# Hybrid encoder block, output part of its ConvFFN: the sums for the last product's weights released one by one during the product s3

## The chip, the cores and the metric

The kernel runs on one core of one Trainium2 chip. The metric is the device time of one execution in microseconds (us); the time of a kernel is the median of its runs. Engines: PE (matmul), PEld (its weight loads), DVE (VectorE), ACT (ScalarE), POOL (GpSimd) and SP (SyncE, here used only to issue transfers).

## What is computed

The reference is a streaming-encoder block on x of 512 x 1024 float32: an RWKV-7 branch and an RG-LRU branch merged by gates, a cross-attention into 256 memory rows, then a gated ConvFFN with inner width 2816, and a last norm. The change touches the ConvFFN's second product, with w_out of 2816 x 1024:

```
def conv_ffn(h, w_in, conv_w, conv_b, w_out):
    u = h @ w_in
    gate = causal_dwconv(u[..., :D_FF], conv_w, conv_b)
    return (jax.nn.gelu(gate) * u[..., D_FF:]) @ w_out

x = x + conv_ffn(rms_norm(x, norm_ffn_g[l]), w_ffn_in[l], ffn_conv_w[l], ffn_conv_b[l], w_ffn_out[l])
return rms_norm(x, norm_final_g)
```

## The kernel before

**The output product in seven products.** The product with w_out is done in Strassen's way (the form with seven products). Its weight matrix is cut into four quarters by input half and output half, its other operand into four quarters by input half and half of the 512 positions. The products run in the order A11, A12, s1, s2, s3, A22, s4 (`out_weights`, L1333). Those with an A take a quarter of w_out itself; those with an s take sums of quarters. Each product has 4 output tiles m times 11 input tiles k = 44 blocks. A block is one 128x128 weight tile against 256 positions. Both factors are split into a high and a low part, and a block is three matmuls (`mm3`, L169 to L173): high by high (L170), high by low (L171), low by high (L172). PSUM tiles are `ox_ps` (X: A11, s2, s3, A22) and `oyz_ps` (YZ: A12, s1, s4).

**The weights of the sums.** They are made in DRAM by transfers, not on an engine: `dO[n, m]` gets one quarter by a copy, and a second one by a transfer that adds to what is there (`accum_op`). POOL's queue issues them (`out_sums`, L518 to L536; the transfers are L521 and L530). s4 has no buffer of its own. Its weights are those of s2 plus one more quarter, added in place in `dO["s2", m]` once the weights of s2 have been read from there:

```
else:
    yield from runs("s2", m, 1, 2, **add)          # L536: n == "s4"
```

`out_runs` cuts a row of 11 blocks wherever a stored piece of 8 blocks ends. For s4 that gives 2, 2, 3 and 2 transfers for m = 0 to 3, nine in all, of 64 to 512 KB, 2816 KB together.

**Pacing.** The generator `sums` (L551) holds all sums of this kind up to s3. `sum_behind(ins)` (L177) takes the next one and lets it wait, by a semaphore, for the matmul `ins`; earlier stages of the kernel call it, and so does the first output product, A11, for its first 12 blocks (L1449). Sums are kept in the order of the program in POOL's queue. The nine sums for s4 are issued by a plain loop between s2 and s3 (L1461), with no pace: each waits only for the loads that read the s2 weights that it overwrites.

**The stream of weights.** `out_weights` packs the 308 blocks of the seven products, in order, into weight tiles of 8 blocks (128x1024, 512 KB). For each of them SP loads a raw tile `wfo_r` (L1354, one transfer or several; four buffers), ACT casts it to the high part `wfo_h` (L1357), DVE makes the low part `wfo_l` (L1358); three buffers each for high and low. Numbered from 0, s2 has tiles 16.5 to 22, s3 22 to 27.5, A22 27.5 to 33, s4 33 to 38.5. Loads of an A product read w_out in DRAM (`in_wfo`), those of an s product read `dO` (shown as `dOs` in the profile).

**Other work around it.** Before a product its second operand is split into high and low by ACT and DVE (`split_g`, L1248 and L1249, tiles `go`); the operand of A22 is built at L1465. As an output tile is finished, DVE and ACT add it to the residual `xr`: s2 at L1460, s3 and A22 and s4 in `ffn_out` (L1395 to L1405).

Of the kernel before, what the change touches and what calls it, by code (L numbers as in the profile page):

```python
# [12 lines left out]
ALU = mybir.AluOpType  # L13
# [45 lines left out]
def hybrid_block_kernel(ctx: ExitStack, tc: tile.TileContext, xT_d, mT_d, pv_d, cst_d, win_d, wk_d, wv_d,  # L59
# [29 lines left out]
    def par(name, i, n=1):  # L89
        o = PV[name][0]  # L90
        return pv[:, o + i:o + i + n]
# [49 lines left out]
    class Units:  # L141
# [10 lines left out]
        def next(self):  # L152
            if self.left == 0:
                self.fill()
            i = self.i
            self.i += 1
            self.left -= 1
            return self.hi[:, i * P:(i + 1) * P], self.lo[:, i * P:(i + 1) * P]
# [10 lines left out]
    def mm3(ps, lh, ll, rh, rl, start, stop, **kw):  # L169
        first = PE.matmul(ps, lh, rh, start=start, stop=False, **kw)  # L170
        PE.matmul(ps, lh, rl, start=False, stop=False, **kw)  # L171
        PE.matmul(ps, ll, rh, start=False, stop=stop, **kw)  # L172
        return first  # L173

    sums = iter(())

    def sum_behind(ins, n=1):  # L177

        for put in islice(sums, n):
            tc.add_manual_dep(tc.keep_in_program_order(put()).ins, ins.ins.name, mybir.DependencyInfo(  # L180
                mybir.DependencyClass.Sync, mybir.DependencyReason.DATA), reason="pace of the sums")
# [293 lines left out]
    def w_sums():  # L475
        def put(b, out, src, acc=True):
            def s(name):
                return dS[b][:, :, SLOT[name], :].rearrange("n p f -> p n f")

            if type(src) is tuple:  # L480
                src = quarter(b * NQ, *src, n=NQ)
            else:
                src = s(src)
            kw = dict(accum_op=ALU.add) if acc else {}
            return lambda: nc.gpsimd.dma_start(s(out), src, **kw)  # L485

        nb = FB // NQ
        for b in range(nb + 1):
            for k in range(4):
                if b < nb:  # L490
                    yield (put(b, "s1", (2, 1), False), put(b, "s1", (2, 2)),
                           put(b, "s3", (2, 1), False), put(b, "s3", (1, 1)))[k]
                if b and k < 2:
                    yield (put(b - 1, "s4", "s2", False), put(b - 1, "s4", (1, 2)))[k]
                elif b < nb and k > 1:
                    yield (put(b, "s2", "s1", False), put(b, "s2", (1, 1)))[k - 2]


    HB = FB // 2
    MQ = KB // 2  # L500

    def out_units(m, r, c):

        return [divmod(((r - 1) * MQ + m) * FB + (c - 1) * HB + k, 8) for k in range(HB)]

    def out_runs(units):

        k = 0
        while k < len(units):
            p, i = units[k]  # L510
            n = min(len(units) - k, 8 - i)
            yield k, n, wfo_d[p, :, i * P:(i + n) * P]
            k += n
# [4 lines left out]
    def out_sums(names):  # L518
        def runs(n, m, r, c, **kw):
            for k, w, src in out_runs(out_units(m, r, c)):  # L520
                yield lambda k=k, w=w, src=src: nc.gpsimd.dma_start(dO[n, m][:, k * P:(k + w) * P], src, **kw)  # L521

        add = dict(accum_op=ALU.add)
        for n in names:
            for m in range(MQ):
                if n == "s1":
                    yield from runs(n, m, 2, 1)
                    yield from runs(n, m, 2, 2, **add)
                elif n == "s2":
                    yield lambda m=m: nc.gpsimd.dma_start(dO["s2", m], dO["s1", m])  # L530
                    yield from runs(n, m, 1, 1, **add)
                elif n == "s3":
                    yield from runs(n, m, 2, 1)
                    yield from runs(n, m, 1, 1, **add)
                else:
                    yield from runs("s2", m, 1, 2, **add)  # L536
# [14 lines left out]
    sums = chain(w_sums(), out_sums(("s1", "s2", "s3")))  # L551
# [189 lines left out]
    with tc.tile_pool(name="pz", bufs=1, reuse_waits="tile") as pz:  # L741
# [9 lines left out]
        for s in range(30, -1, -1):  # L751
            n = 31 - s
# [25 lines left out]
    for i0 in (0, 16):  # L778
# [3 lines left out]
        for i in range(16):  # L782
            for e in range(2):
                r, k = rows[0][e], rows[1][e]
                PE.matmul(psh[e][k, i * 32:(i + 1) * 32], BZ[r, i0 + i, 32:64], ZA[r, i0 + i, :],
                          start=True, stop=True)
        for e, copy in enumerate((S.copy, V.tensor_copy)):
            k = rows[1][e]
            copy(Hs[e][k], psh[e][k].rearrange("p (i t) -> p i t", t=32))
        for i in range(16):  # L790
            for e in range(2):
                r, k = rows[0][e], rows[1][e]
                PE.matmul(pso[e][r, i * 32:(i + 1) * 32], Hs[e][k, i, :], BZ[k, i0 + i, 32:64],
                          start=True, stop=True)
# [384 lines left out]
    for m in order:  # L1179
# [5 lines left out]
        i = m % 4  # L1185
# [60 lines left out]
    def split_g(i, src, k):  # L1246
        dst, n = part(i, k)
        S.copy(dst[:, :, 0, :], src(slice(k, k + n)))  # L1248
        V.tensor_tensor(dst[:, :, 1, :], src(slice(k, k + n)), dst[:, :, 0, :].bitcast(F32), ALU.subtract)  # L1249

    def g1(ks, c):
        return graw[:, ks, (c - 1) * H:c * H]
# [15 lines left out]
    for m0 in range(0, FB, NQ):  # L1268
        ms = range(m0, m0 + NQ)
        YZ = {m: pf.tile([P, T], F32, tag="yz", name=f"fyz_ps{m}", bufs=4) for m in ms}  # L1270
        X = {m: pf.tile([P, T], F32, tag="x", name=f"fx_ps{m}", bufs=4)[:, 0:H] for m in ms}
        sn = {m: pc.tile([P, T], F32, tag="sn", name=f"sn{m}", bufs=3) for m in ms}
        p5 = {m: pc.tile([P, H], F32, tag="p5", name=f"p5_{m}", bufs=3) for m in ms}
# [14 lines left out]
        elif m0 // NQ <= KB:  # L1288
            k = m0 // NQ - 1
# [13 lines left out]
        for m in ms:  # L1303
# [9 lines left out]
            out = graw[:, m]  # L1313
            V.scalar_tensor_tensor(out[:, 0:H], X[m], -1.0, ac[:, 0:H], ALU.mult, ALU.mult)
            V.scalar_tensor_tensor(out[:, H:T], p5[m], -1.0, ac[:, H:T], ALU.mult, ALU.mult)
            k = m % HB
# [44 lines left out]

    uf = out_weights()

    def out_product(n, i, out, start, done, nsum=0):

        for m, k in out_order:
            wh, wl = next(uf)
            g = gsets[i][k // 8][:, k % 8]
            ins = mm3(out[m], wh, wl, g[:, 0, :], g[:, 1, :], start and k == 0, k == HB - 1,
                      skip_group_check=not start)  # L1370
            if m * HB + k < nsum:
                sum_behind(ins)
            if k == HB - 1:
                done(m)
# [9 lines left out]
    X = [pf.tile([P, T], F32, tag="x", name=f"ox_ps{m}", bufs=4)[:, 0:H] for m in range(MQ)]  # L1384
    YZ = [pf.tile([P, T], F32, tag="yz", name=f"oyz_ps{m}", bufs=4) for m in range(MQ)]
    cols = (slice(0, H), slice(H, T))
    sn1, sn5 = ([pc.tile([P, T], F32, tag="sn", name=f"{n}_{i}", bufs=3) for i in range(2)] for n in ("o1", "o5"))
    p1, p5 = ([t[:, c] for t in ts for c in cols] for ts in (sn1, sn5))

    def ffn_out(src, snap, sign, m, ts, last=False):  # L1390

        n = ts.stop - ts.start
        if snap is not None:
            t1 = pc.tile([P, T], F32, tag="s", name=f"t1_{m}_{ts.start}")
            V.tensor_tensor(t1[:, :n], src, snap, ALU.add)  # L1395
            src = t1[:, :n]
        V.tensor_tensor(xr[:, m, ts], xr[:, m, ts], src, sign)
        sq = pc.tile([P, T], F32, tag="ac", name=f"t2_{m}_{ts.start}")[:, :n]
        S.activation(sq, xr[:, m, ts], AF.Square)
        if last:  # L1400
            V.tensor_scalar(xr[:, m, ts], xr[:, m, ts], par("nfin", m), None, ALU.mult)
        else:
            S.activation(xr[:, m, ts], xr[:, m, ts], AF.Identity, scale=par("nfin", m))
        if not last:
            V.tensor_tensor(sso[:, ts], sso[:, ts], sq, ALU.add)  # L1405
        return sq
# [40 lines left out]
    prepare(1, lambda ks: g2(ks, 1))  # L1447
    prepare(2, lambda ks: g1(ks, 1))
    out_product("A11", 0, X, True, lambda m: S.copy(p1[m], X[m]), 12)  # L1449
    for k in K4:  # L1450
        ks = slice(k, min(k + 4, HB))
        V.scalar_tensor_tensor(g1(ks, 1), g2(ks, 2), -1.0, g1(ks, 1), ALU.mult, ALU.subtract)
        split_g(0, lambda ks: g1(ks, 1), k)
    out_product("A12", 1, [t[:, 0:H] for t in YZ], True,
                lambda m: ffn_out(YZ[m][:, 0:H], p1[m], ALU.add, m, cols[0]))
    prepare(1, lambda ks: g2(ks, 2))
    out_product("s1", 2, [t[:, H:T] for t in YZ], True, lambda m: S.copy(p5[m], YZ[m][:, H:T]))
    prepare(2, lambda ks: g1(ks, 2))
    out_product("s2", 0, X, False,
                lambda m: V.tensor_tensor(xr[:, m, cols[1]], xr[:, m, cols[1]], X[m], ALU.add))  # L1460
    for put in out_sums(("s4",)):  # L1461
        tc.keep_in_program_order(put())
    for k in K4:
        ks = slice(k, min(k + 4, HB))
        V.scalar_tensor_tensor(g1(ks, 1), g1(ks, 1), -1.0, g2(ks, 1), ALU.mult, ALU.subtract)  # L1465
        split_g(0, lambda ks: g1(ks, 1), k)
    out_product("s3", 2, X, False, lambda m: ffn_out(X[m], p5[m], ALU.subtract, MQ + m, cols[1]))
    out_product("A22", 0, X, False, c21)
    out_product("s4", 1, [t[:, H:T] for t in YZ], False, c12)

# [76 lines left out]
```

## Time and profile before

| | us |
|---|---|
| timed runs | 885.95, 889.65, 891.37 |
| median | 889.65 |
| profiled execution, its own time | 888.2 |
| its span, first to last instruction | 886.4 |
| PE busy | 865.9 (98%) |
| DVE busy | 676.7 (76%) |
| ACT busy | 513.6 (58%) |
| POOL busy | 132.5 (15%) |

Times in the profile are us from the start of the span. A row of instructions gives start, duration, engine, line, operation, output <- inputs, and in brackets the idle time of the engine before it with what ended that. A matmul lasts longer than the distance to the next one, since matmuls are pipelined: the pace is read from the starts. Transfers have a time to landing, from issue until their data is in place. Queue q0 is POOL's, q1 is SP's; they share 16 DMA engines.

### The profile page before, as it was taken

To read this page: it belongs to the slowest core of one execution; us is meant where nothing else is said; L and a number is where in the kernel's file an instruction comes from. 1 tells how busy PE (TensorE), PEld (TensorE's weight loads), DVE (VectorE), ACT (ScalarE), POOL (GpSimd) and SP (SyncE) were. 2 spreads that over 40 slices of the span, in tenths; PEclk is the share of its full clock that TensorE was granted. 3 is DMA by queue.
4 is the path that set the end of the run, shared out by engine and by line. 5 is a ranking of instruction groups with operands and counts; after the bars stand their busy time and mean duration, and the time that the engine had idled before them with its cause. 6 is when DMAs were issued, how large, how long until landed. Compare 5 with 4: busy or idle time off the path is not lost.

```text
span 886.4 us, 15940 instructions
## 1 busy us (share of the span) xinstructions
PE 865.9 (98%) x6197; PEld 755.0 (85%) x6197; DVE 676.7 (76%) x1096; ACT 513.6 (58%) x788; POOL 132.5 (15%) x163
## 2 busy tenths in 40 slices
PE   8999999999999999999989999999999999999996
PEld 7778878888877677888867778999999999999896
DVE  6796598777967777685565568898888788998674
ACT  7575676643337676243454456766665566767563
POOL 0101222021101012001112211112111211111100
PEclk9999999999999999999999999999999999999999
DMA  8878899678997379858877868899999999998963
GB/s 279 301 254 215 209 223 238 191 197 240 260 236 156 74 197 230 229 157 239 220 205 169 203 150 191 239 258 285 300 257 297 262 320 277 249 280 207 293 208 95
DMA packets 97562, 201.37 MB, mean 227 GB/s; under 512 B 19600, under 2 KB 30992, under 8 KB 97424
## 3 DMA queue, kind: packets, MB, share of 16 engines
q1 hardware_dynamic: 62240, 118.57, 40.5%
q0 software_dynamic: 25504, 67.38, 37.3%
q10 hardware_dynamic: 9744, 14.42, 4.9%
q8 instruction: 48, 0.79, 0.4%
q14 instruction: 26, 0.21, 0.1%
HBM read 188.54 MB, written 78.12 MB: 301 GB/s over the span
## 4 chain that ended last, share of the span: by engine, by line
PE 80%; DMA 8%; DVE 7%; ACT 3%; issue 1%; ACTq 0%; SPq 0%; DVEq 0%
PE in_ps L171 7%; PE in_ps L172 7%; PE in_ps L170 7%; PE fx_ps L170 3%; PE fx_ps L172 3%; PE fx_ps L171 3%; PE fyz_ps L170 3%; PE fyz_ps L171 3%; PE fyz_ps L172 3%; DMA wfi_r<-in_wfi 2%; DMA wfo_r<-dOs 2%; PE co_ps L172 2%; PE mix_ps L171 2%; PE co_ps L171 2%; PE mix_ps L170 2%; PE co_ps L170 2%
## 5 line engine op out<-in xcount | busy, mean ns | idle before, releaser
L171 PE MATMUL in_ps<-hT,win_h 128*128 128x512 f32 x304 | 121.0, 398 | 0.4 <-DVE hT L387 0.4
L172 PE MATMUL in_ps<-hT,win_l 128*128 128x512 f32 x304 | 121.3, 399 | 0.0
L170 PE MATMUL in_ps<-hT,win_h 128*128 128x512 f32 x304 | 120.5, 398 | 0.3 <-DVE pr L589 0.3
L136 ACT CAST wfi_h<-wfi_r 128x1024 fp32r<-128x1024 f32 x77 | 80.9, 1051 | 64.4 <-PE fyz_ps L171 17.2
L137 DVE TENSOR_TENSOR wfi_l<-wfi_r,wfi_h 128x1024 fp32r<-128x1024 f32 x77 | 93.9, 1220 | 23.5 <-ACT wfi_h L136 23.4
L485 POOL DMA_DIRECT2D dS<-in_wfi x66 | 66.7, 1034 | 299.2 <-PE in_ps L170 96.4
L171 PEld LDWEIGHTS in_ps<-hT,win_h 128*128 128x128 f32 x304 | 57.1, 188 | 14.6 <-DVE hT L387 1.0
L170 PEld LDWEIGHTS in_ps<-hT,win_h 128*128 128x128 f32 x304 | 57.1, 188 | 13.4 <-DVE pr L589 0.7
L172 PEld LDWEIGHTS in_ps<-hT,win_l 128*128 128x128 f32 x304 | 57.1, 188 | 12.9 <-issue 0.7
L521 POOL DMA_DIRECT2D dOs<-in_wfo x54 | 39.8, 784 | 171.3 <-PE fx_ps L170 46.0
L123 DVE TENSOR_TENSOR win_l<-win_r,win_h 128x1024 fp32r<-128x1024 f32 x38 | 46.3, 1220 | 24.1 <-ACT win_h L122 20.6
L122 ACT CAST win_h<-win_r 128x1024 fp32r<-128x1024 f32 x38 | 39.9, 1050 | 40.0 <-PE in_ps L171 35.6
L1358 DVE TENSOR_TENSOR wfo_l<-wfo_r,wfo_h 128x1024 fp32r<-128x1024 f32 (+1 forms) x39 | 46.9, 1206 | 14.4 <-ACT wfo_h L1357 14.4
L1357 ACT CAST wfo_h<-wfo_r 128x1024 fp32r<-128x1024 f32 (+1 forms) x39 | 40.3, 1035 | 30.3 <-DMA wfo_r<-dOs 14.0
L172 PE MATMUL ox_ps<-go,wfo_l 128*128 128x256 f32 x176 | 48.8, 277 | 1.2 <-DVE wfo_l L1358 1.2
L170 PE MATMUL ox_ps<-go,wfo_h 128*128 128x256 f32 x176 | 48.7, 277 | 0.6 <-ACT wfo_h L1357 0.6
L170 PE MATMUL fx_ps<-hr,wfi_h 128*128 128x256 f32 x176 | 48.7, 277 | 0.3 <-ACT sn L1293 0.3
L170 PE MATMUL fx_ps<-hq,wfi_h 128*128 128x256 f32 x176 | 48.8, 277 | 0.1
L172 PE MATMUL fyz_ps<-hq,wfi_l 128*128 128x256 f32 x176 | 48.7, 277 | 0.0
L172 PE MATMUL fx_ps<-hq,wfi_l 128*128 128x256 f32 x176 | 48.7, 277 | 0.0
L170 PE MATMUL fyz_ps<-hq,wfi_h 128*128 128x256 f32 x176 | 48.7, 277 | 0.0
L171 PE MATMUL fx_ps<-hq,wfi_h 128*128 128x256 f32 x176 | 48.6, 276 | 0.0
(432 smaller groups left out, 2689.7 us busy)
## 6 DMA issues: line engine op xcount, KB each, us to landing
dS<-in_wfi POOLq DMA_DIRECT2D x66, 512.0 KB, 7.6
wfi_r<-dS SPq DMA_DIRECT2D x44, 512.0 KB, 6.9
win_r<-in_win SPq DMA_DIRECT2D x38, 512.0 KB, 5.3
wfi_r<-in_wfi SPq DMA_DIRECT2D x33, 512.0 KB, 5.6
dS<-dS POOLq DMA_DIRECT2D x22, 512.0 KB, 5.7
dOs<-in_wfo POOLq DMA_DIRECT2D x12, 512.0 KB, 7.8
wk_r<-in_wk SPq DMA_DIRECT2D x8, 512.0 KB, 5.8
wv_r<-in_wv SPq DMA_DIRECT2D x8, 512.0 KB, 5.2
```

The lines of the kernel that those rows point to most:

```text
L122: casts.append(S.copy(hi[:, o:o + n], raw[:, o:o + n]))
L123: V.tensor_tensor(lo[:, o:o + n], raw[:, o:o + n], hi[:, o:o + n].bitcast(F32), ALU.subtract)
L136: S.copy(hi, raw)
L137: V.tensor_tensor(lo, raw, hi.bitcast(F32), ALU.subtract)
L170: first = PE.matmul(ps, lh, rh, start=start, stop=False, **kw)
L171: PE.matmul(ps, lh, rl, start=False, stop=False, **kw)
L172: PE.matmul(ps, ll, rh, start=False, stop=stop, **kw)
L485: return lambda: nc.gpsimd.dma_start(s(out), src, **kw)
L521: yield lambda k=k, w=w, src=src: nc.gpsimd.dma_start(dO[n, m][:, k * P:(k + w) * P], src, **kw)
L1357: S.copy(hi[:, :n], raw[:, :n])
L1358: V.tensor_tensor(lo[:, :n], raw[:, :n], hi[:, :n].bitcast(F32), ALU.subtract)
```

## The change

The nine sums for s4 are no longer issued between s2 and s3. They are put behind what is left in `sums`, and the product s3 releases them: `out_product` gets an argument `every`, and with `every=3` the blocks 0, 3, 6, ... of s3, counted over its 44 blocks, release one sum each, until `nsum` have been released. `nsum` is `len(late)`, the count of the sums for s4, nine by the code above, so block 24 releases the last. What would be left in `sums` then is issued after s3. The short description of the change speaks of ten transfers; the code gives nine.

```
-    def out_product(n, i, out, start, done, nsum=0):
+    def out_product(n, i, out, start, done, nsum=0, every=1):
...
-            if m * HB + k < nsum:
+            if (m * HB + k) % every == 0 and (m * HB + k) // every < nsum:
                 sum_behind(ins)
...
-    for put in out_sums(("s4",)):
-        tc.keep_in_program_order(put())
+    late = list(out_sums(("s4",)))
+    sums = chain(sums, late)
     for k in K4:
         ks = slice(k, min(k + 4, HB))
         V.scalar_tensor_tensor(g1(ks, 1), g1(ks, 1), -1.0, g2(ks, 1), ALU.mult, ALU.subtract)
         split_g(0, lambda ks: g1(ks, 1), k)
-    out_product("s3", 2, X, False, lambda m: ffn_out(X[m], p5[m], ALU.subtract, MQ + m, cols[1]))
+    out_product("s3", 2, X, False, lambda m: ffn_out(X[m], p5[m], ALU.subtract, MQ + m, cols[1]),
+                len(late), 3)
+    for put in sums:
+        tc.keep_in_program_order(put())
```

## Prediction

> **What bounds the kernel now.** I read the summary of busy time first, then the busy time by stretches of the output part, then PE's own instructions there, then the chain of work that ended last, and at the end the queue of POOL and the transfers.
>
> ```profile
> span 886.4 us, 15940 instructions
> ## 1 busy us (share of the span) xinstructions
> PE 865.9 (98%) x6197; PEld 755.0 (85%) x6197; DVE 676.7 (76%) x1096; ACT 513.6 (58%) x788; POOL 132.5 (15%) x163
> ```
>
> PE is busy for 98% of the span. A change that takes no matmul away can give back PE's idle time and nothing else, so the question is how much of that idle time lies where the nine transfers run. The stretches of the output part (columns: stretch, its length, then PE, PEld, DVE, ACT, POOL busy, granted clock, DMA share, GB/s) say:
>
> ```profile
> 769.00:784.00 15.00, 15.00 (x135) 15.00 (x134) 15.00 (x20) 10.00 (x14) 3.31 (x5) 1.00 1.00 297
> 784.00:799.00 15.00, 15.00 (x135) 15.00 (x134) 14.85 (x17) 10.62 (x13) 1.67 (x2) 1.00 0.91 260
> 799.00:815.00 16.00, 16.00 (x141) 15.90 (x141) 15.78 (x21) 12.98 (x22) 2.45 (x3) 1.00 0.74 182
> 815.00:833.00 18.00, 16.65 (x144) 16.25 (x143) 10.03 (x12) 7.93 (x9) 4.91 (x6) 1.00 1.08 281
> 833.00:848.00 15.00, 14.57 (x129) 14.38 (x128) 13.39 (x20) 9.49 (x13) 0.00 (x0) 1.00 0.87 278
> 848.00:863.00 15.00, 15.00 (x132) 14.87 (x130) 9.67 (x16) 9.89 (x15) 0.00 (x0) 1.00 0.65 198
> ```
>
> PE is full in these stretches but for 815 to 833 (1.35 us idle, most of s2) and 833 to 848 (0.43 us, s3). In the first of these the DMA share is 1.08: the sixteen engines have no free time. PE's own rows give the loss exactly:
>
> ```profile
> 814.01 0.28 PE L170 MATMUL ox_ps<-go,wfo_h 128*128 128x256 f32 x1
> ...
> 823.20 0.28 PE L170 MATMUL ox_ps<-go,wfo_h 128*128 128x256 f32 x1
> ...
> 824.29 0.38 PE L170 MATMUL ox_ps<-go,wfo_h 128*128 128x256 f32 x1 [0.59 <-ACT wfo_h L1357]
> ...
> 830.92 0.28 PE L170 MATMUL ox_ps<-go,wfo_h 128*128 128x256 f32 x1
> ...
> 861.58 0.60 PE L1411 MATMUL rs_ps<-sso,onesr 128*128 128x256 f32 x2
> ```
>
> 814.01 is the first matmul of s2 and 823.20 that of its block 27, so a block of three matmuls takes (823.20 - 814.01) / 27 = 0.3404 us, a product of 44 blocks 14.98 us, and one weight tile (8 blocks) 2.72 us. s3 begins at 830.92, after 16.91 us instead of 14.98: **1.93 us lost in s2**. From there to 861.58, the end of A22, lie 30.66 us for 88 blocks that need 29.96: **0.70 us lost in s3 and A22**. Together 2.63 us, 0.3% of the span. That is all that this stretch can give.
>
> Why s2 stalls is in the chain of waits:
>
> ```profile
> 810.43 1.15 DVE wfo_l L1358
> 811.60 0.32 SPq L1354
> 812.01 11.08 DMA wfo_r<-dOs
> 823.19 1.05 ACT wfo_h L1357
> ```
>
> The stall at 824.29 is at block 28 of s2, the first block of weight tile 20. Its load was issued at 811.60, took 11.08 us, was cast in 1.05 us, and PE was already waiting. Two things came together. First, the load was issued late: a raw buffer (four of them) comes free when the low part of the tile four places earlier is made. That is made when PE starts the tile two places before it (three buffers), so the load of tile 20 belongs about 1.2 us after PE starts tile 14 (at 807.2, six tiles of 2.72 us before 823.5), near 808.4. It came 3.2 us late, since DVE was full (15.78 of 16 us in 799 to 815). Second, it took 11.08 us. What filled the engines is POOL's queue:
>
> ```profile
> 808.59 1.64 POOL L521 DMA_DIRECT2D dOs<-in_wfo  x2 [22.37 <-DMA wfo_r<-dOs]
> 811.09 0.81 POOL L521 DMA_DIRECT2D dOs<-in_wfo  x1 [0.86 <-issue]
> 815.28 0.80 POOL L521 DMA_DIRECT2D dOs<-in_wfo  x1 [3.38 <-DMA wfo_r<-dOs]
> 818.56 0.81 POOL L521 DMA_DIRECT2D dOs<-in_wfo  x1 [2.47 <-DMA wfo_r<-dOs]
> 821.98 2.48 POOL L521 DMA_DIRECT2D dOs<-in_wfo  x3 [2.61 <-DMA wfo_r<-dOs]
> 824.99 0.81 POOL L521 DMA_DIRECT2D dOs<-in_wfo  x1 [0.53 <-DMA wfo_r<-dOs]
> 880.25 1.41 POOL L1428 TENSOR_TENSOR xr<-xr,ro 128x256 f32<-128x256 f32 x2 [54.44 <-ACT ro L1425]
> ```
>
> These are the transfers of the change: 2+1+1+1+3+1 = 9 (not ten), each released as soon as the s2 weights that it overwrites have been read. Loads beside them and clear of them, from the lists of transfers of four stretches (769 to 784, 815 to 826, two rows of 833 to 848, 848 to 863; last number: us to landing, or share of the engines for a queue):
>
> ```profile
> wfo_r<-in_wfo SPq DMA_DIRECT2D x1, 512.0 KB, 5.3
> ...
> wfo_r<-dOs SPq DMA_DIRECT2D x1, 512.0 KB, 10.6
> ...
> q0 software_dynamic: 55, 0.16, 5.5%
> ...
> wfo_r<-in_wfo SPq DMA_DIRECT2D x1, 512.0 KB, 4.1
> ...
> wfo_r<-dOs SPq DMA_DIRECT2D x2, 512.0 KB, 4.4
> ```
>
> A 512 KB load takes 10.6 us beside the nine, 4.1 to 4.4 clear of them. POOL's queue (q0) has 5.5% of the engines in 833 to 848, 0.8 us of the sixteen, so the nine end near 834: about 25 us from 808.6.
>
> **The change, part by part.** It issues the same nine transfers, of the same size, from the same queue; nothing is added to or removed from PE, ACT, DVE or SP. Each gets one more wait, for the first matmul of block 0, 3, ..., 24 of s3.
>
> *What goes.* Without the nine in 808 to 829, the load of tile 20, still late at 811.6, lands after about 4.4 us, at 816.4. Cast (1.05) and low part (1.15) are done by 819, before PE needs them at 823.5. Every later load of s2 and s3 is earlier too. So s2 loses its 1.93 us, s3 starts at 814.01 + 14.98 = 829.0, and the loss in s3, which follows from tiles late in the same stretch, goes as well: between 1.93 and 2.63 us; I take 2.5.
>
> *Where they go.* Block 0 of s3 is at 829.0 and block 24 at 829.0 + 24 x 0.3404 = 837.2. The nine are offered within 8.2 us instead of 16.4, and occupy the engines from 829 to about 854 if they again need 25 us. Behind the waiting instruction on POOL stand only the other eight and the product at 880.25, which waits 54 us for ACT anyway. The old condition, that the s2 weights have been read, let the last transfer go at 824.99; it is met before 829 and costs nothing.
>
> *Who meets them there.* The loads of A22 (tiles 27.5 to 32) and the first of s4. Their cost is not seen in this trace, so I bound it. One raw buffer goes round in issue 0.32 + landing + 1.05 + 1.15 us, and four of them feed PE. With 4.1 us of landing that is 6.6 us for four tiles, against 10.9 that PE needs: free. With 10.6 us it is 13.1, or 3.28 us a tile against 2.72, a deficit of 0.56 us for each of 25 / 3.28 = 7.6 tiles: 4.3 us. The two finished tiles ahead of PE are a lead of 2 x 2.72 = 5.4 us. So with DVE in time the deficit is covered; with the 3.2 us of lateness of tile 20 it is 4.3 + 3.2 - 5.4 = 2.1 us, which is near the 1.93 that s2 lost, and so bears the model out. At s3 DVE has 13.39 of 15 us of work, and its three splits of A22's operand fall there:
>
> ```profile
> L1249 DVE TENSOR_TENSOR go<-graw,go x9: 946/1214/1225, 801.9 to 837.0; 128x1024 fp32r<-128x1024 f32 x6, 128x768 fp32r<-128x768 f32 x3
> ```
>
> Two of 1.21 us and one of 0.95 are 3.4 us; they can hold a low part up by one or two of them, so I put the lateness at 1 to 1.5 us: 4.3 + 1.5 - 5.4 = 0.4. Bounds: 0 (below that nothing: 848 to 863 has no stall to lose) and, with 11.08 us of landing all through and 3.2 us of lateness, 3.40 us a tile, 0.68 x 7.4 = 5.0, and 5.0 + 3.2 - 5.4 = 2.8. The nearest row is 769 to 784: loads from the same source beside five sums on POOL, a full DVE, 5.3 us for 512 KB, and PE 15.00 of 15. I take 0.5 us.
>
> On this point the Trainium skill (DMA: Bandwidth & Descriptors, section Queues, rings and completion order) says that each DMA engine takes turns between the queues that have work, a packet at a time. By that the collision only moves, and A22's loads land as late as those of s2 did; this trace agrees that the queues share, with 10.6 us against 4.4, and the sum by it would be the second rival's.
>
> *Who waits for them.*
>
> ```profile
> 847.72 14.14 SPq L1354 DMA_DIRECT2D wfo_r<-dOs  x9
> ```
>
> s4's first load, of tile 33, is issued at 847.7, about 845.2 after the change; tile 37, the first that needs the last transfer, 4 x 2.72 later at 856.1. The nine are through by 854. PE needs tile 37 near 861.6 - 2.5 + 10.9 = 870, and load, cast and low part take 7 us, so the cover holds to 863.
>
> *Sum.* -2.5 + 0.5 = **-2.0 us**. The profiled execution took 888.2 us (span 886.4), giving 886.2. The three timed runs are 885.95, 889.65 and 891.37; with the profiled one their mean is 888.8, and I set the forecast against that: **886.8 us**. One per cent (8.9 us) is about what a measurement of this kernel can tell from no change, and the sum is far below it.
>
> **The rivals.**
>
> *The stall stays.* If DVE's lateness alone made the stall of s2, moving the transfers gains nothing: 888.8. For it: DVE full before 815. Against it: the cast of tile 20 began when its load landed, at 823.19, 11.08 us after the issue; with 4.4 us the lateness of 3.2 is covered.
>
> *The collision moves.* The nine cost A22 what they cost s2: 2.1 us against 2.5 gained, -0.4 us: 888.4. For it: the same engines, the same transfers, offered twice as densely. Against it: 769 to 784 without a stall, and DVE less full.
>
> *The weights of A22 come too late, and it is slower.* Place: the raw buffers, while the nine run beside tiles 28 to 34. Price: the 2.8 us of the upper bound, against only 1.93 gained: +0.9, or 889.7. It decides from a landing of about 11 us with a lateness near 3 us. Waiting for s4's sums would be added only if the last of them landed after 863, 9 us later than I expect; each us beyond costs one.
>
> *It does not do what it says.* The transfers could bunch behind PE and stay as dense as now. That changes nothing by itself, since the engines are full either way: it falls under the second rival. A different order of instructions elsewhere, by the scheduler, could move the time by a few us either way.
>
> **How the numbers follow.** Forecast (a gain of 1 to 2.6 us) 0.50; the collision moves 0.22; the stall stays 0.08; slower by A22 0.14; a shift of order elsewhere 0.06. All but the last lie within 3 us of 888.8. The timed runs scatter by 2.8 us around it, more than the cases do. Low end: 886.8 less that scatter, 884. High end: the slower case with scatter, 889.7 + 1.8 = 891.5. Faster by over 1% would need 8.9 us, over three times the idle time of PE here: 0.02. Slower by over 1% needs s4 to wait or a worse order: 0.03. Within 1%: 0.95.
>
> **What would show it.** On PE: s2 from its first matmul to s3's in 15.0 us, with no wait for ACT or DVE; then s3 and A22 in 30.0 to 30.9 us. On SP: 512 KB loads from 808 to 826 in 4 to 6 us, those from 830 to 850 in 8 to 11. On POOL: nine transfers about 1.02 us apart, each released by PE's s3. On ACT: waits for the loads of A22 where there are few now. A stall in A22 of over 2 us would make the forecast wrong, and so would one at the start of s4; a change on PE before 808 would say that the order of the program, not the transfers, has moved the time.

## Result and the profile after

The changed kernel takes 892.96 us in the median of 19 runs, the kernel before 888.39 us in 19 runs on the same chip: a ratio of 1.0037, 95% interval 1.0021 to 1.0053. It is 3.3 us slower by this ratio (1.9 to 4.7); the ratio is not the quotient of the two medians, which lie 4.6 us apart. That is within 1%, as expected, but on the other side, and above the range of 884 to 891.5.

The page of the changed kernel and its output part, product by product (s2, s3, A22; columns as before):

```profile
span 891.8 us, 15944 instructions
## 1 busy us (share of the span) xinstructions
PE 871.3 (98%) x6197; PEld 760.5 (85%) x6197; DVE 677.6 (76%) x1096; ACT 512.7 (57%) x788; POOL 132.4 (15%) x163
```

```profile
817.43:832.39 14.96, 14.96 (x134) 14.96 (x133) 10.64 (x13) 8.51 (x10) 0.00 (x0) 1.00 0.74 231
832.39:847.35 14.96, 14.96 (x134) 14.96 (x133) 10.91 (x16) 6.81 (x10) 7.28 (x9) 1.00 1.01 207
847.35:867.23 19.88, 16.67 (x136) 15.64 (x135) 11.75 (x17) 11.31 (x18) 0.00 (x0) 1.00 0.93 269
```

The borders are the first matmuls of the products, from PE's rows of the changed kernel:

```profile
817.43 0.28 PE L170 MATMUL ox_ps<-go,wfo_h 128*128 128x256 f32 x1
...
832.39 0.28 PE L170 MATMUL ox_ps<-go,wfo_h 128*128 128x256 f32 x1
...
847.35 0.28 PE L170 MATMUL ox_ps<-go,wfo_h 128*128 128x256 f32 x1
...
866.99 0.60 PE L1411 MATMUL rs_ps<-sso,onesr 128*128 128x256 f32 x2
```

s2 and s3 run at full pace, 14.96 us each; before, s2 took 16.91. A22 takes 19.6 us up to the row L1411, against 14.98 without a stall: 4.7 us are lost there. From the first matmul of s2 to the first of s4 the changed kernel needs 49.80 us, the kernel before needed 47.82: +2.0 us.

POOL's queue did what the change says (first and last of the nine rows):

```profile
832.97 0.81 POOL L521 DMA_DIRECT2D dOs<-in_wfo  x1 [41.89 <-DMA wfo_r<-dOs]
...
841.13 0.81 POOL L521 DMA_DIRECT2D dOs<-in_wfo  x1 [0.21 <-issue]
```

Nine transfers, 1.02 us apart. The chain of waits of the changed kernel shows who paid:

```profile
840.23 0.35 DVE sso L1405
840.62 0.43 SPq L1354
841.10 15.34 DMA wfo_r<-in_wfo
856.54 1.05 ACT wfo_h L1357
857.62 1.24 DVE wfo_l L1358
858.90 0.38 PE ox_ps L172
```

A load of A22 takes 15.34 us to land, and PE waits for its low part. The transfers while the sums run, in the kernel before (808 to 836) and in the changed one (833 to 855); for a queue: packets, MB, share of the 16 engines:

```profile
q0 software_dynamic: 1294, 2.88, 59.0%
q1 hardware_dynamic: 1930, 4.50, 44.4%
```

```profile
q0 software_dynamic: 1293, 2.88, 75.5%
q1 hardware_dynamic: 1400, 2.00, 29.1%
...
wfo_r<-in_wfo SPq DMA_DIRECT2D x1, 320.0 KB, 15.3
```

The sums are the same 2.88 MB. The loads beside them fell from 4.50 MB in 28 us (161 GB/s) to 2.00 MB in 22 us (91 GB/s). PE needs 512 KB in 2.72 us, 193 GB/s. **This is where the loss in A22 comes from: the weights come at half the pace that PE eats them.** That nothing else adds to it is shown by the runs without the sums (e1) and with plain copies (e7) below.

The rest of the distance between these two profiles does not come from the output part. Of the 5.4 us between the spans 3.1 lie before the output part (A11 starts at 768.91 before, 771.98 after), where all instructions are in the same order in both kernels. There PE's granted clock (third number from the end) fell in the attention, in 456 to 464, first before, then after:

```profile
456.00:464.00 8.00, 5.57 (x33) 4.85 (x34) 5.43 (x16) 4.97 (x12) 1.68 (x2) 1.00 0.71 143
```

```profile
456.00:464.00 8.00, 5.10 (x19) 4.72 (x20) 3.50 (x10) 4.32 (x10) 0.84 (x1) 0.62 0.75 145
```

That the change has no part in this is argued, not shown: over the fourteen profiles of this case, all with the same order of instructions up to there, A11 starts anywhere from 766.1 to 772.0.

### The profile page after: what moved, and what is told of

Its sections match the earlier page's. It is cut to its first block, busy times and chain, and to the rows that moved or that the text cites. A ratio compares the mean times of both kernels' runs of the same rounds, so it can differ in the third digit from the quotient of the medians.

```text
span 891.8 us, 15944 instructions
## 1 busy us (share of the span) xinstructions
PE 871.3 (98%) x6197; PEld 760.5 (85%) x6197; DVE 677.6 (76%) x1096; ACT 512.7 (57%) x788; POOL 132.4 (15%) x163
## 4 chain that ended last, share of the span: by engine, by line
PE 78%; DMA 10%; DVE 6%; ACT 3%; issue 1%; ACTq 0%; SPq 0%; DVEq 0%
PE in_ps L171 7%; PE in_ps L170 7%; PE in_ps L172 7%; DMA wfi_r<-dS 3%; PE fx_ps L170 3%; PE fx_ps L172 3%; PE fx_ps L171 3%; PE fyz_ps L170 2%; PE fyz_ps L172 2%; PE fyz_ps L171 2%; DMA wfi_r<-in_wfi 2%; PE oyz_ps L172 2%; DMA wfo_r<-in_wfo 2%; PE oyz_ps L171 2%; PE oyz_ps L170 2%; PE mix_ps L170 2%
## 5 line engine op out<-in xcount | busy, mean ns | idle before, releaser
L170 PE MATMUL fyz_ps<-hq,wfi_h 128*128 128x256 f32 x176 | 48.8, 277 | 0.0
L171 PE MATMUL fyz_ps<-hq,wfi_h 128*128 128x256 f32 x176 | 48.6, 276 | 0.0
```

## Experiments

The measure is PE's time from the first matmul of s2 to the first of s4, read from PE's rows, besides the timed ratio to the kernel before. Two theories stood against each other for the stalls of A22. **Pace**: nine sums in 8 us instead of 16 leave the loads no room. **Kind of loads**: A22's loads, from w_out in many small pieces, lose more beside sums than those of s3, which read whole rows.

**No sums (e1).** `late = []` in place of the list of the sums.

> The nine sums for s4 are left out (s4 then works with the weights of s2); all else as in the changed kernel. Measure: PE from the first matmul of s2 to the first of s4 (before 47.8 us, changed kernel 49.8; 132 blocks of 0.3404 us and a little make 45.2). If the nine transfers make all of the stalls, whatever the way: 45.2 us, no wait of PE in s2, s3 or A22, and 2.6 us less than before in time. If something else of the change (the order of instructions, the waits on PE) costs time: over 46 us.

45.13 us, no wait of PE; ratio 0.9946 (0.9915 to 0.9976). The nine transfers make all of the stalls of both kernels, and nothing else in the change costs time. DVE is as full ahead of s2 as it was before (15.82 of 16 us, against 15.78; the stretch lies as far behind the start of A11, which is 2.8 us earlier here):

```profile
796.20:812.20 16.00, 16.00 (x140) 15.79 (x139) 15.82 (x22) 13.03 (x20) 0.00 (x0) 1.00 0.63 202
```

45.13 us is the floor for the table below.

**The same pace, earlier (e2).** Sums are given a block of their own, whose first matmul they wait for:

```
+            blocks.append(ins)
+            while late and late[0][0] < len(blocks) and len(blocks) > 176:
+                at, put = late.pop(0)
+                tc.add_manual_dep(tc.keep_in_program_order(put()).ins, blocks[at].ins.name, ...)
...
+    late += zip(range(148, 173, 3), out_sums(("s4",)))
```

> The nine sums are released at the same pace as in the changed kernel, one every third block, but by blocks 16, 19, ..., 40 of s2, so that they run beside the loads of s3 (whole rows from the sum buffers) instead of those of A22 (pieces of w_out). Density theory (nine in 8 us instead of 16 are what starves the loads): 512 KB loads of s3 land after 11 to 15 us, PE from s2 to s4 takes about 49.8 us as in the changed kernel. Theory of the kind of loads (A22's loads, in more and smaller pieces, lose more beside the sums): landings of 11 us or less, and 47.8 us or less.

49.69 us: as bad as the changed kernel, but half of the stalls, 2.3 us, lies in s3 and the other half in A22, since the sums (the nine issued from 819.8 to 829.0, through by 846.6) met both. The list of transfers of 820 to 843:

```profile
wfo_r<-dOs SPq DMA_DIRECT2D x1, 512.0 KB, 11.5
```

By the bounds that I had set, both the landing of 11.5 us and the 49.69 us speak for the pace: at one sum every third block loads of whole rows starve as well. It is no clean test, since half of the stall fell on loads of A22. The timed ratio, 1.0002 (0.9975 to 1.0029), is lower than that of the changed kernel, but the intervals overlap.

**A22's loads from whole rows (e3, repeated as e11 beside the changed kernel, e12).** In `out_weights`, before the case of the A products:

```
+                if n == "A22":
+                    flat.append(((n, m), dO["s3", m], k))
```

> As the changed kernel, but the loads of A22 read the sum buffers of s3 (whole rows, 9 transfers) instead of w_out (13 pieces); A22 then works with other weights. Density theory: the kind of load does not matter, landings of 11 to 15 us and about 49.8 us from s2 to s4. Theory of the kind of loads: landings of 11 us or less, 47.5 us or less, and a time below before.

> The kernel with A22's loads from whole rows once more, beside the changed kernel on the same chip. If the kind of loads makes the difference between the changed kernel and before: 48 to 49.5 us from s2 to s4 and a time like before, 2 to 4 us below the changed kernel. If it does not: 50 us or more, and a time like the changed kernel's.

> The changed kernel, for the comparison on the same chip: 49.5 to 52 us from s2 to s4, stalls in A22 alone, and a time 2 to 5 us above before.

48.35 us (ratio 1.0004, 0.9967 to 1.0041) and 50.25 us (1.0013, 0.9990 to 1.0036), the changed kernel 49.85 us (1.0044, 1.0025 to 1.0064). In e11 a drop of PE's clock after the stall, told of below, is in the 50.25 us and costs over 1 us of it. The transfers of the first 20 us from the first sum on, e11 (827.8 to 847.8) first, then e12 (831.7 to 851.7):

```profile
q0 software_dynamic: 1115, 2.34, 68.7%
q1 hardware_dynamic: 1118, 2.36, 34.5%
```

```profile
q0 software_dynamic: 1221, 2.64, 76.1%
q1 hardware_dynamic: 1222, 1.75, 28.2%
```

In the same 20 us the loads from whole rows brought 2.36 MB in fewer packets (2.11 KB each), the pieces of w_out 1.75 MB (1.43 KB each). So the kind of loads matters for the bytes, and probably for the time: with whole rows it comes to about that of before, 2.8 us below the changed kernel on the same chip, but the intervals still overlap. The stretch from s2 to s4 does not settle it: 48.35 us lies between the bounds of the two theories, and 50.25 us, clock drop included, is what I had expected if the kind made no difference. It does not remove the stall either: both profiles stay 3 us and more above the floor, and the longest landings of loads from whole rows are 14.4 and 14.7 us, against 15.4 in e12. The landings under 11 us and the 47.5 us of my expectation were missed.

**A wider pace at the same place (e4).** `len(late), 5` in place of `len(late), 3`.

> As the changed kernel, but every fifth block of s3 releases a sum: 1.7 us apart instead of 1.02, block 0 to 40, 13.6 us instead of 8.2. Density theory: landings near 10.6 us and 48 us or less from s2 to s4. Theory of the kind of loads: the engines are full all the same, landings of 11 us and more, 49 to 50 us, the stalls a little later in A22.

50.48 us, with a drop of PE's clock in it (23 matmuls in 856 to 860 instead of 35; by that count about 1.4 us). Without it the stretch would take about 49 us, an estimate, hardly less than the 49.80 of the changed kernel; ratio 1.0026 (0.9996 to 1.0057). From 831 to 855:

```profile
q0 software_dynamic: 1296, 2.88, 68.8%
q1 hardware_dynamic: 1900, 2.87, 35.9%
```

68.8% of 24 us over nine sums is 1.8 us of all sixteen engines for each. At 1.7 us apart the sums leave no gap, so this run varied the pace less than it was meant to: the 48 us of the density theory were missed, but that does not refute it.

**The distances of before, in s3 (e6).** As e2, with blocks 0, 2, 7, 20, 29, 39 and 41 of s3, 0 and 4 of A22.

> The nine sums at the distances that they had before (0, 0.8, 2.5, 6.7, 10, 13.4, 14.2, 15.2, 16.4 us), but from the first block of s3 on: blocks 0, 2, 7, 20, 29, 39 and 41 of s3, 0 and 4 of A22. Pace theory: the distances make the cost, so s2 to s4 takes 47.8 us as before. Place theory: 49.5 us or more as with every third or fifth block, since the loads of A22 are the weaker ones.

47.72 us, the number of the pace theory. But this profile is no repeat of the kernel before. These are PE's waits at the end of A22 and in s4, and then two stretches of s4 (columns as before):

```profile
862.31 0.70 PE L1418 MATMUL rs_ps<-sso,onesr 128*128 128x256 f32 x2 [1.96 <-DVE sso L1412]
864.82 1.22 PE L1419 MATMUL rs_ps<-t,onesr 128*128 128x256 f32 x2 [0.57 <-ACT t L1406]
```

```profile
863.00:867.00 4.00, 3.43 (x17) 2.95 (x16) 2.77 (x5) 2.30 (x5) 0.00 (x0) 0.55 0.50 165
867.00:871.00 4.00, 4.00 (x23) 4.00 (x23) 3.08 (x5) 1.05 (x1) 0.00 (x0) 0.59 0.62 205
```

The first wait lies just before the first matmul of s4 (862.66) and is in the 47.72: a late weight tile held DVE, behind it the end of A22, and behind that PE. A drop of the clock followed, to 0.55 and 0.59, and with the second wait s4 took 19.04 us instead of 15.54. From the first block of s2 to the last of s4 it is 66.8 us, against 63.4 before and 65.4 after in the first profiles. This execution took 892.49 us, 3.1 us more than the median of e6, so it is not typical. By the timed ratio, 0.9999 (0.9972 to 1.0025), e6 is as fast as the kernel before, on the chip where the changed kernel took 1.0037 (1.0015 to 1.0059, e8 below). The two intervals overlap a little. So in time the sums at the distances of before cost about what they cost before, beside the loads of A22 too; whether a part of the stall moved on to s4 in the other executions is not shown.

**Plain copies (e7).** `yield from runs("s2", m, 1, 2)` without `**add`.

> As the changed kernel, but the nine transfers overwrite instead of adding up (s4 then works with one quarter of the weights): the same bytes from the same source at the same place and pace, without the read of the destination. If the cost is that a packet of a sum holds an engine for some 0.28 us, against 0.10 for a packet of a load, while the two queues take turns: the loads get twice as much, land within 9 us, and s2 to s4 takes 45.2 to 47 us. If the number of transfers or their bytes make the cost: 49 us or more.

45.13 us, no stall, and no load landed later than 8.8 us; ratio 0.9971 (0.9953 to 0.9989), which overlaps with the ratio without sums. From 829 to 850:

```profile
q1 hardware_dynamic: 2302, 3.68, 53.8%
q0 software_dynamic: 752, 2.88, 39.0%
```

The same 2.88 MB need 39.0% of 21 x 16 = 131 us of engine time as copies, and 75.5% of 22 x 16 = 266 us as sums, in 752 packets and 1293. A packet of a sum held an engine for 266 / 1293 = 0.21 us (I had put 0.28), one of A22's loads for 29.1% x 352 / 1400 = 0.07 us. It is the adding that fills the engines, not the bytes.

**Sums far apart (e5).** As e2, with blocks 0, 13 and 28 of s2, 2, 12, 15, 35 and 40 of s3 and 4 of A22.

> The nine sums of the changed kernel, released by blocks 0, 13 and 28 of s2, 2, 12, 15, 35 and 40 of s3 and 4 of A22: about 31 us from the first to the last release, one every 3 to 7 us by its size, so that POOL's transfers are through before the next is released. Gap theory (what counts is whether the queue of the sums runs empty between two of them, which it does at 3 to 7 us but neither at 1.0 nor at 1.7): 512 KB loads land within 9 us, PE from the first matmul of s2 to the first of s4 takes 45.2 to 46.5 us, and the time is 1 to 2.6 us below before. Place theory (beside the loads of A22 the sums always cost 4 us or more): over 47.8 us, since half of them still run there.

45.14 us, the floor; PE is full in all three stretches, and three whole tiles of 512 KB land in 4.6 us (the median; 7.6 us is the longest of any load beside the sums). The transfers are those of 814 to 858:

```profile
812.00:827.00 15.00, 15.00 (x135) 15.00 (x134) 10.67 (x13) 8.55 (x11) 2.42 (x3) 1.00 0.98 270
827.00:842.00 15.00, 15.00 (x135) 15.00 (x134) 12.67 (x18) 10.09 (x14) 3.76 (x5) 1.00 1.00 262
842.00:857.00 15.00, 15.00 (x135) 15.00 (x134) 10.38 (x15) 8.58 (x14) 1.09 (x2) 1.00 0.95 280
```

```profile
q1 hardware_dynamic: 4396, 8.63, 55.5%
q0 software_dynamic: 1296, 2.88, 40.3%
...
wfo_r<-dOs SPq DMA_DIRECT2D x3, 512.0 KB, 4.6
```

The loads get 8.63 MB in 44 us, 196 GB/s: what PE needs. The median is 884.56 us, a ratio of 0.9951 (0.9931 to 0.9972) to the kernel before. **This version beats both kernels**, and is as fast as no sums at all (0.9946); by its ratio it gains 4.4 us (2.5 to 6.1), more than the 1 to 2.6 us that I expected.

The sums are 3.4 to 6.8 us apart, and 1.0, 1.7 and 2.7 us behind the three small ones of 64, 128 and 192 KB. The same 2.88 MB, the same adding and in part the same loads of A22 cost nothing here, so the place theory is out. Two readings are left that these runs do not separate: that the queue of the sums must run empty in between, or only that over this length both queues fit (55.5% and 40.3% of the engines, together 96%; in the changed kernel 75.5% and 29.1% fill them, and the loads still fall short).

**The two kernels again (e8, e9, e10).**

> The changed kernel once more, to see how far its profile varies: s2 without a stall, 49 to 50.5 us from s2 to s4, stalls in A22 alone; the first matmul of the output part between 766 and 772 us, at random.

> The kernel before once more, for its profile: 47 to 49 us from the first matmul of s2 to the first of s4. If stalls of s2 sometimes bring the clock of PE down, as those of A22 did in two of three profiles at a dense pace, it shows here as a stretch of some 3.4 us at half clock after 824 us; if only the longer stalls do it, there is none.

> The same once more: 47 to 49 us from s2 to s4, with or without a stretch of some 3.4 us at half clock.

| PE from s2 to s4, us | profiles |
|---|---|
| floor (e1, e5, e7) | 45.13, 45.14, 45.13 |
| before (first, e9, e10) | 47.82, 48.67, 49.47 |
| changed (first, e8, e12) | 49.80, 51.56, 49.85 |

e8 timed 1.0037 (1.0015 to 1.0059). e8 and e10 have a drop of PE's clock in them (last section) and lie above the ranges that I expected. Above the floor the kernel before loses 3.5 us in the mean of three, the changed one 5.3.

## Why the prediction was wrong

**What went: right, and a little small.** s2 took 14.96 us and s3 14.96, with no wait, where I said 15.0 and none. The stall of s2 came from the sums alone: e1 removes it with DVE as full as before; so the first rival, that the stall stays, is out. I took 2.5 us from one profile; three gave 2.7, 3.5 and 4.3, the last with a drop of the clock.

**Where they go: right.** Nine transfers, 1.02 us apart, each released by s3, the last at block 24; the nine are through within about 22 us, where I said 25; in the kernel before it was 28 us, to 836.4 and not to 834.

**Who meets them there: the step that failed.** I put the cost in A22 at 0.5 us, 2.8 at most. It was 4.7 us in the first profile. The frame of that step, four raw buffers going round and a lead of two tiles, needs one input, the landing, and that was mis-sized: I took 10.6 us, 11.08 at most, from loads beside sums at the distances of before; the loads of A22 took up to 15.3. By the formula of that step 0.43 + 15.34 + 1.05 + 1.24 is 18.1 us for four tiles, 4.5 us a tile against 2.72, a deficit of 1.8 us for each of 22 / 4.5 = 4.9 tiles: 8.8 us. With the same lateness of 1 to 1.5 us and the same lead of 5.4 that makes 4.4 to 4.9 us. It takes the longest landing for every load, so it bears the frame out only roughly; but the size of the landing alone is enough to make the loss.

Two things lengthened the landing. The first is the pace, nine sums in 8 us instead of 16: at it, loads of whole rows took up to 14.4 and 14.7 us too (e3, e11), and at the distances of before the loads of A22 took 9.8 us at most (e6). The second is the kind of loads (e11 and e12), which makes less of the longest landings: 15.4 us against 14.7. My nearest row, 5.3 us beside five sums in 769 to 784, was no likeness: by the order and the sizes in `out_sums` three of those five (448, 384 and 320 KB) are plain copies of s3's first quarter, and e7 shows that copies need half the engine time.

On the second rival, that the collision only moves, the runs agree in kind: it moved, and it became dearer by coming denser. The third rival's side came out, by its mechanism (the weights of A22 late) but beyond its price: +0.9 us forecast, 3.3 us measured. The two queues in the changed kernel, in 836 to 840 and in 842 to 854:

```profile
q0 software_dynamic: 243, 0.63, 100.6%
q1 hardware_dynamic: 4, 0.00, 0.3%
```

```profile
q0 software_dynamic: 875, 1.73, 77.3%
q1 hardware_dynamic: 887, 1.21, 32.6%
```

From 842 on the two queues come out nearly even in packets. The Trainium skill (DMA: Bandwidth & Descriptors, section Queues, rings and completion order) gives this taking of turns, on which I had weighed this rival; the twelve us agree with it, if the packets of the profile are those of the page. e11 and e12 show what I left out of it: taking turns by the packet, a queue of small packets loses bytes to a queue of long ones. In 836 to 840 it did not hold: loads had been issued from 835.8 on, and for 4 us SP's queue moved next to nothing, while the sums filled the engines. With sums every 1.0 and 1.7 us the same shows in e3 and e4 (19 and 0 packets of loads in 833 to 837). A small load can land 1.8 us after its issue when no sum runs, so starting up does not account for it. Why it happens, and how much of the 4.7 us it makes, is open.

**Who waits for them: right.** s4 took 15.56 us from its first matmul, 15.54 before; no load of s4 waited so long for a sum that PE did.

**The sum.** s3 and A22 lost 4.64 us (34.60 from 832.39 to 866.99, against 29.96) instead of 0.70, s2 none instead of 1.93: +2.0 us by the first profiles. The timed difference is 3.3 us (1.9 to 4.7). The three profiles of each kernel give 1.8 us in the mean and scatter by 1.8 within a kernel, so some 1.5 us of it is not accounted for. Part of it may lie before the output part, where A11 starts at 769.0 us in the mean of the three profiles before and at 770.8 after; whether that and the rest are chance or more drops of the clock is open.

The range was also narrower than its own terms: its low end takes off the whole scatter of 2.8 us, its high end adds 1.8. With 2.8 it would have ended at 892.5, still below the median measured.

## What to carry to other kernels

Spreading transfers out helped here when each had time to end, over nearly all of the stretch that the data allow; nine in 8 or 14 us, without a gap between them, cost as much as before or more. So first work out the engine time of one (here 1.8 us of all sixteen for a sum, in the mean) and add up what both queues need over the stretch. A transfer that adds up took about twice the engine time of a copy here, and the loads beside it lost more when they were cut into small pieces. A stall that is removed by moving its cause has to be paid for at the new place, at the new distances and with that place's own loads, not with the old place's landing time. And a row that serves as the nearest likeness should be checked for what its transfers do: copies are not sums.

## What was not expected of the hardware

A drop of PE's clock can follow short stalls. In e8 PE waited four times for 0.3 to 0.8 us each around 852 to 859 and then ran at about half the clock; the same in the kernel before (e10) after the stall of s2:

```profile
852.00:859.00 7.00, 4.71 (x34) 4.11 (x35) 4.16 (x7) 3.13 (x5) 0.00 (x0) 1.00 0.91 315
859.00:863.00 4.00, 4.00 (x24) 4.00 (x23) 3.01 (x5) 3.40 (x6) 0.00 (x0) 0.57 0.82 255
863.00:867.00 4.00, 4.00 (x38) 4.00 (x37) 2.81 (x4) 1.89 (x4) 0.00 (x0) 1.00 0.75 211
```

```profile
824.00:828.00 4.00, 2.09 (x16) 1.70 (x15) 1.81 (x3) 2.22 (x3) 2.71 (x4) 1.00 1.10 335
828.00:832.00 4.00, 4.00 (x23) 4.00 (x23) 2.49 (x3) 0.92 (x1) 0.00 (x0) 0.57 1.10 239
832.00:836.00 4.00, 4.00 (x37) 4.00 (x37) 2.56 (x3) 2.95 (x3) 0.00 (x0) 1.00 1.06 284
```

PE shows as busy in the middle row, but with 24 matmuls in 4 us instead of 35: at a granted clock of 0.57, about a third of the 4 us is lost, over 1 us on top of the stall. From s2 on such a drop came in five of the fourteen profiles (e4, e6, e8, e10, e11), each time after stalls, and not in others of the same kernel. The same two stretches as of e8, in the first profile of the changed kernel:

```profile
852.00:859.00 7.00, 4.53 (x33) 3.73 (x31) 3.37 (x5) 3.19 (x5) 0.00 (x0) 1.00 1.02 329
859.00:863.00 4.00, 4.00 (x35) 4.00 (x36) 3.84 (x7) 3.77 (x7) 0.00 (x0) 1.00 0.73 213
```

The Trainium skill (TensorE: Matmul & The Clock Gate, Part 1) gives half the clock after an idle window of about 3.4 us; here PE was never idle for that long at once. In e8 the drop followed 2.3 us of idle time in 7. The amount alone does not decide: the rows above have 2.5 us of idle time in the same 7 and no drop. What does is open.
